# Building scratch sums in DRAM beside a projection: 1 MB accumulating DMAs with 8 KB rows, one in every second group, and copies seven to eight groups behind their sums

## The chip, the cores and the metric

One core of a Trainium2 chip. The time is the device time of one execution in microseconds (us); several executions are timed and the median is compared.

## The reference

One layer of a streaming encoder over 2048 prompt tokens and 64 sample tokens, float32, width 1024. Cut to what matters here:

```python
a = rmsnorm(h, norm1)
qa, ka, va, qr, kr, vr, gr = project(a, w_in)      # one projection, attention and retention columns
mixed = concat(window_attention(qa, ka, va), group_norm(retention(qr, kr, vr)) * silu(gr))
h = h + mixed @ w_out
u = relu(rmsnorm(h, norm2) @ w_up)                 # 1024 -> 4096
h = h + (u * u) @ w_down                           # 4096 -> 1024
y = rmsnorm(h, norm_f)
```

## The kernel before

The work has four stages, one after the other on TensorE.

1. **First projection with attention and retention.** Tokens are in tiles of 128 (17 tiles, the last of 64). The heads are done in two halves, `ph` 0 and 1, and for each half all tiles are gone through. A tile has three *groups* of matmuls (`ci` 0, 1, 2; lines 527, 528, 530), 102 groups in all; between the matmuls of a group stand the attention and retention steps of earlier tiles. The first and last tiles of each half are taken in pairs. The order on TensorE and on SyncE is written out by hand (`manual_schedule` for these two); that of the other engines is fixed when the program is built.
2. **Output projection** with residual and norm.
3. **Up projection** (`up_pair`, lines 856 to 858).
4. **Down projection** (lines 1025 to 1027) and last norm.

The two MLP products are done in the Strassen-Winograd way: weights and activations are cut into 2 x 2 blocks, and seven products of sums of blocks take the place of eight. For this, four sums of weight blocks are needed, with L11, L12, L21, L22 the blocks of a weight matrix: S1 = L21 + L22, S3 = L11 + L21, S2 = S1 + L11, S4 = S2 + L12. They do not depend on the tokens, and they are formed during stage 1 in DRAM scratch, `uscr` for w_up and `sscr` for w_down: a plain copy of one block into the scratch, issued from SyncE (line 585), and then an accumulating DMA that adds the other block to it, issued from GpSimd (POOL, line 588). Four copies and four sums make one unit; a unit is 512 KB of each sum, and there are 16.

`sum_step` has six steps for each unit, and the group loop calls them after the group with the number `first + 4 * u + 2 * k`:

- k = 0: copies S1 <- L21 and S3 <- L11; k = 1: sums S1 += L22, S3 += L21
- k = 2: copy S2 <- S1; k = 3: sum S2 += L11
- k = 4: copy S4 <- S2; k = 5: sum S4 += L12

So units overlap: away from the ends, every fourth group has four copies of 512 KB behind it, and two groups later there are four sums. On GpSimd a sum is placed behind the last rotation (`last_pool`, the addition of line 197). A copy that reads a sum (S2 <- S1, S4 <- S2) waits for it on SyncE, and a sum waits on GpSimd for the copy that it adds to.

On the same SyncE queue are, in program order, the loads of the next tiles: `load_x` (line 143, `xr`, one buffer), and `load_aux` (line 161, `rt`, the rotary table, two buffers; line 164, `xk`, the tokens for the norm, one buffer, in half 0 only). ScalarE squares `xk` (line 165) and splits `xr` into `xh` (line 154), GpSimd makes `xl` (line 155). GpSimd also forms `es` (line 291), the sink term of the softmax, which ScalarE then exponentiates (line 292).

In stages 3 and 4 `up_weights` (line 838) and `left` read single blocks from the weights and sums from the scratch. `wup` is laid out in 32 pieces of 128 rows of 1024 numbers, `uscr` in pieces of 128 rows of 512; `wdn` in 32 pieces `[128, 8, 128]`, by eights in one DMA; `sscr` in rows of 2048.

Of the kernel before, what the change touches and what calls it, by code (L numbers as in the profile page):

```python
# [11 lines left out]
F32 = mybir.dt.float32  # L12
F32R = mybir.dt.float32r
AF = mybir.ActivationFunctionType
ALU = mybir.AluOpType
# [24 lines left out]
def body(ctx, tc, xt, xtok, w1, wout, wup, wdn, gains, sinks, ck, cv, sret, rot, rdec, qdec, dmask,  # L40
         yT, nkp, nvp, nrp, nks, nvs, nrs):
    nc = tc.nc
# [3 lines left out]
    dp = ctx.enter_context(tc.tile_pool(name="scratch", bufs=1, space=DR))  # L46
# [3 lines left out]
    hscr = dp.tile([NK, 128, NTOK], F32, name="hscr")  # L50
    ascr = dp.tile([NP, 7, 128, 4, NB], F32, name="ascr")
    vscr = dp.tile([NP, 7, 128, 16, NB], F32, name="vscr")
    uscr = dp.tile([4, 16, 128, 512], F32, name="uscr")
    sscr = dp.tile([4, 4, 128, 2048], F32, name="sscr")

    idf = cp.tile([128, 128], F32, name="idf")
# [41 lines left out]
    last_pool = [None]  # L98
# [444 lines left out]
    S = NT - 1  # L543
# [8 lines left out]
    a, b = tiles[:2]  # L552
# [15 lines left out]
    def blocks(u):  # L568


        if u < 8:
            j = slice(2 * u, 2 * u + 2), slice(2 * u + 16, 2 * u + 18)
            return [uscr[k, j[0]].rearrange("j p c -> p j c") for k in range(4)], \
                [wup[e, :, c:c + 512].rearrange("j p c -> p j c") for e in j for c in (0, 512)]
        d, c = (u - 8) // 2, (u - 8) % 2 * 1024
        return [sscr[k, d, :, c:c + 1024] for k in range(4)], \
            [wdn[e].rearrange("p f n -> p (f n)")[:, a + c:a + c + 1024] for e in (d, d + 4) for a in (0, 2048)]

    def sum_step(u, k):

        (S1, S2, S3, S4), (L11, L12, L21, L22) = blocks(u)
        copies, sums = {0: ([(S1, L21), (S3, L11)], ()), 1: ((), [(S1, L22), (S3, L21)]), 2: ([(S2, S1)], ()),
                        3: ((), [(S2, L11)]), 4: ([(S4, S2)], ()), 5: ((), [(S4, L12)])}[k]
        for dst, src in copies:
            nc.sync.dma_start(dst, src)
        with tc.issue_after(last_pool[0].ins):
            for dst, src in sums:
                nc.gpsimd.dma_start(dst, src, accum_op=ALU.add, max_dma_last_dim=4096)

    first = groups.index((0, 2, 0))  # L590
    sums = {}
    for u in range(16):
        for k in range(6):
            sums.setdefault(first + 4 * u + 2 * k, []).append((u, k))
    aux = []

    for i, (ph, t, ci) in enumerate(groups):
# [13 lines left out]
        if aux and aux[0][0] <= i:  # L611
            u = aux.pop(0)[1]
# [32 lines left out]
    def rawslot(name):  # L645
        return wr.tile([128, 1024], F32, name=name, tag="wr")
# [7 lines left out]
    def split(h, l, x):  # L654
        nc.scalar.activation(h, x, AF.Copy)  # L655
        sub(l, x, h.bitcast(F32))  # L656
# [36 lines left out]
    RIGHT = {1: 0, 2: 1, 3: 2, 5: 3, 7: 4, 6: 5, 4: 6}  # L693

    LEFT = {5: 0, 6: 1, 7: 2, 3: 3}


    def load_mix(p, f):
# [46 lines left out]
    def norm_part(p, slot):  # L745

        n = Norm()

        def split():
            r, t = (slot(*x).rearrange("p (a n) t -> p a (n t)", a=2) for x in (("nr", F32R), ("nt", F32)))  # L750
            n.split(rs2[:, p * PN:p * PN + PN], accs[p], (r[:, 0], r[:, 1]), (t[:, 0], t[:, 1]))
        return split, n.sums, n.power
# [41 lines left out]
    with pool(name="op", bufs=1, side="right") as op:  # L794
# [7 lines left out]
        n = norm_part(0, opslot)  # L802
# [11 lines left out]
        n = norm_part(1, opslot)  # L814
# [17 lines left out]
    def up_weights(j):  # L832
        src = {}
        for n, i in enumerate(ORDER):
            if n % 2 == 0:
                r = rawslot("upr")
            x = r[:, n % 2 * 512:n % 2 * 512 + 512]
            nc.sync.dma_start(x, wup[j, :, :512] if i == 1 else wup[j, :, 512:] if i == 2 else
                              wup[j + 16, :, 512:] if i == 4 else uscr[LEFT[i], j])
            src[i] = x  # L840
        return src

    def up_pair(p, j, after):
        src = up_weights(j)
        a, b, c = psum("a"), psum("b"), zp.tile([128, 512], F32, name="c", tag="z")
        bank = {1: a, 2: a, 6: b, 7: b, 4: b, 5: c, 3: c}
# [65 lines left out]
    def left(i, d):  # L912

        out = []
        for g in range(2):
            r = rawslot("dr")
            if i in (1, 2, 4):
                e, a = d + 4 * (i == 4), 16 * (i != 1) + 8 * g
                nc.sync.dma_start(r.rearrange("p (f n) -> p f n", f=8), wdn[e, :, a:a + 8])
            else:  # L920
                nc.sync.dma_start(r, sscr[LEFT[i], d, :, g * 1024:g * 1024 + 1024])
            w = wd.tile([128, 2, 1024], F32R, name="wd", tag="wd")
            split(w[:, 0], w[:, 1], r)
            out.append(w)
        return out
# [78 lines left out]
    prods = [(p, i) for p in range(NP) for i in DOWN]  # L1004
    R = {prods[0]: [right(0, DOWN[0], c) for c in range(4)]}
    W = {steps[0]: left(*steps[0][1:])}
    pending = {}
    for n, (p, i, d) in enumerate(steps):
# [6 lines left out]
        if n + 1 < len(steps):  # L1015
            W[steps[n + 1]] = left(*steps[n + 1][1:])
# [36 lines left out]
        if last and i in (5, 3):  # L1053
            q = 22 if i == 5 else 12
            g = 4 * (q // 10 - 1) + d
# [29 lines left out]
def _rot_table():  # L1085
    pos = np.arange(NTOK).astype(np.float32)[:, None]
    out = []
    for f in (_FA, _FR):
        ang = (pos * f[None, :]).astype(np.float32).astype(np.float64)
        c, s = np.cos(ang), np.sin(ang)  # L1090
        out += [c, c, -s, s]
    return np.ascontiguousarray(np.concatenate(out, axis=1).astype(np.float32))


def _decay_tables():
    lg = _LOG_G.astype(np.float64)
    i = np.arange(128.0)
    rd = np.zeros((128, 2, 4))
    for a, C in enumerate((128, 64)):
        rd[:, a, :] = np.exp(lg[None, :] * (C - 1 - i)[:, None]) * 128.0 ** -0.5  # L1100
    qd = np.broadcast_to(np.exp(lg[:, None] * (i + 1)[None, :])[None], (128, 4, 128))
    causal = (i[None, :] >= i[:, None]).astype(np.float64)
    dm = np.concatenate([causal[:, None, :] * np.exp(-lg * C)[None, :, None] for C in (128, 64)], axis=1)
    return [np.ascontiguousarray(a.astype(np.float32)) for a in (rd, qd, dm)]
# [5 lines left out]
def _arrays(x_prompt, x_sample, cache_k, cache_v, state_ret, norm1, w_in, sinks, w_out, norm2, w_up, w_down, norm_f):  # L1110
    f = np.ascontiguousarray
    xa = np.concatenate([np.asarray(x_prompt)[0], np.asarray(x_sample)[0]], axis=0)
    xt = f(xa.T.reshape(8, 128, NTOK).transpose(1, 0, 2))
    w = np.asarray(w_in)[0]
    phs = []
    for ph in range(2):
        cols = [np.arange(640 + 64 * ph, 704 + 64 * ph),
                np.arange(256 * ph, 256 * ph + 256),
                np.arange(512 + 64 * ph, 576 + 64 * ph)]
        for b in (768, 1280, 1792, 2304):  # L1120
            cols.append(np.arange(b + 256 * ph, b + 256 * ph + 256))
        wp = w[:, np.concatenate(cols)]
        phs.append(wp.reshape(8, 128, WP).transpose(1, 0, 2))
    w1 = f(np.stack(phs, 0))
    wup = f(np.asarray(w_up)[0].reshape(8, 128, 32, 128).transpose(2, 1, 0, 3).reshape(32, 128, 1024))
    wout = f(np.asarray(w_out)[0].reshape(8, 128, 8, 128).transpose(2, 1, 0, 3).reshape(8, 128, 1024))
    wdn = f(np.asarray(w_down)[0].reshape(32, 128, 8, 128).transpose(2, 1, 0, 3))
    gains = f(np.stack([np.asarray(a).reshape(8, 128).T for a in (norm1, norm2, norm_f)], axis=1))
    sk = np.asarray(sinks)[0].reshape(2, 2, 2)
    sk = np.repeat(sk.transpose(2, 0, 1), 64, axis=0)  # L1130
    sk = f(np.concatenate([sk, sk], axis=2))
    rd, qd, dm = _decay_tables()
    return dict(xt=xt, xtok=f(xa), w1=w1, wout=wout, wup=wup, wdn=wdn,
                gains=gains, sinks=sk, ck=f(np.asarray(cache_k)[0, 0]), cv=f(np.asarray(cache_v)[0, 0]),
                sret=f(np.asarray(state_ret)[0, 0]), rot=_rot_table(), rdec=rd, qdec=qd, dmask=dm)
# [21 lines left out]
```

## Time and profile before

| | |
|---|---|
| median of 3 runs | 2346.11 us (2345.71 to 2350.67) |
| the profiled execution | 2352.45 us, its span 2350.7 us |
| busy share of the span | PE 95%, DVE 63%, ACT 47%, POOL 21% |
| DMA traffic | 515.91 MB, mean 219 GB/s |
| queue of SyncE (q1) | 470.21 MB, 59.5% of the DMA engines' time |
| queue of GpSimd (q0) | 43.43 MB, 10.0% |
| sums, `uscr` and `sscr` | 32 + 32 of 512 KB, median 10.8 and 10.9 us from issue to landing |
| granted TensorE clock | 0.973 of full speed |

Lines of the profile name the engine: PE is TensorE's matmul, PEld its weight load, ACT ScalarE, DVE VectorE, POOL GpSimd, SP SyncE; a q behind the name is that engine's instruction queue. `out<-in` are the program's names for tiles. In brackets stands how long the engine was idle before the instruction, and what ended that. "DMA to landing" is the time from the issue of a DMA to its completion. A busy engine costs time only where the chain of work passes through it, so the profile is read by stretches of time: the 40 slices of the page are 59 us each, and stage 1 fills the first 14.

### The profile page before, as it was taken

How to read it: one execution, taken by the hardware profiler on the slowest of the kernel's cores; microseconds unless marked ns; L12 is line 12 of the kernel's file. 1: busy time of each engine (PE TensorE's matmuls, PEld its weight loads, DVE VectorE, ACT ScalarE, POOL GpSimd, SP SyncE). 2: the span in 40 equal slices, each digit the busy share in tenths (PEclk: the TensorE clock that was granted, in tenths of full speed). 3: DMA queues.
4: the chain of work that ended last, by engine and by line, in shares of the span. 5: the costliest groups of instructions: out<-in, count | busy, mean ns of one | idle time of the engine just before them, and what ended most of it. 6: DMA issues, size and time to landing. Idle time of an engine off the chain costs nothing.

```text
span 2350.7 us, 35610 instructions
## 1 busy us (share of the span) xinstructions
PE 2241.2 (95%) x13256; PEld 2134.7 (91%) x13256; DVE 1469.8 (63%) x2460; ACT 1115.4 (47%) x1982; POOL 485.2 (21%) x582
## 2 busy tenths in 40 slices
PE   7978888898999989999999999999999999999998
PEld 5867777787888879999999999999999999999998
DVE  5544444554445565768768767766756776687665
ACT  5433333443334353345556556655644444444452
POOL 5544454443333322210000000000000110020012
PEclk9999898899999989999999999999999999999999
DMA  6557769885731277958979967876886677678762
GB/s 188 141 122 189 167 158 226 215 198 145 162 84 46 66 234 239 339 166 292 343 239 317 362 220 264 297 240 229 294 283 227 227 279 267 225 279 282 236 213 79
DMA packets 254766, 515.91 MB, mean 219 GB/s; under 512 B 22353, under 2 KB 128017, under 8 KB 254593
## 3 DMA queue, kind: packets, MB, share of 16 engines
q1 hardware_dynamic: 237312, 470.21, 59.5%
q0 software_dynamic: 17280, 43.43, 10.0%
q8 instruction: 104, 1.70, 0.3%
q14 instruction: 70, 0.57, 0.1%
HBM read 411.19 MB, written 169.54 MB: 247 GB/s over the span
## 4 chain that ended last, share of the span: by engine, by line
PE 83%; DMA 8%; ACT 2%; DVE 2%; POOL 2%; issue 1%; SPq 1%; DVEq 0%; POOLq 0%; ACTq 0%
PE y L1026 9%; PE y L1027 9%; PE y L1025 9%; PE z L527 5%; PE z L528 5%; PE z L530 4%; PE b L856 4%; PE b L857 4%; PE b L858 4%; DMA xk<-in_xtok 3%; PE y L731 3%; PE y L732 3%; PE c L856 3%; PE a L856 3%; PE a L857 3%; PE y L733 3%
## 5 line engine op out<-in xcount | busy, mean ns | idle before, releaser
L1026 PE MATMUL y<-vl,wd 128*128 128x352 f32 x1344 | 438.3, 326 | 0.0
L1027 PE MATMUL y<-vh,wd 128*128 128x352 f32 x1344 | 436.1, 324 | 1.3 <-DVE wd L656 1.3
L1025 PE MATMUL y<-vh,wd 128*128 128x352 f32 x1344 | 433.8, 323 | 2.7 <-ACT wd L655 2.7
L527 PE MATMUL z<-w,xh 128*128 128x512 f32 (+1 forms) x816 | 333.7, 409 | 12.3 <-ACT w L86 7.5
L976 POOL TENSOR_TENSOR acc<-acc,sq 128x352 f32<-128x352 f32 x41 | 73.0, 1780 | 1221.0 <-ACT sq L972 1221.0
L528 PE MATMUL z<-w,xh 128*128 128x512 f32 (+1 forms) x816 | 316.2, 387 | 1.3 <-DVE w L87 1.3
L655 ACT ACTIVATE wd<-dr 128x1024 fp32r<-128x1024 f32 x168 | 177.1, 1056 | 257.3 <-PE y L1027 187.7
L530 PE MATMUL z<-w,xl 128*128 128x512 f32 (+1 forms) x768 | 293.9, 383 | 1.6 <-POOL xl L155 1.6
L655 ACT ACTIVATE wu<-upr 128x512 fp32r<-128x512 f32 x336 | 209.4, 627 | 175.8 <-PE b L858 83.2
L656 DVE TENSOR_TENSOR wd<-dr,wd 128x1024 fp32r<-128x1024 f32 x168 | 209.3, 1247 | 110.8 <-ACT wd L655 103.0
L656 DVE TENSOR_TENSOR wu<-upr,wu 128x512 fp32r<-128x512 f32 x336 | 230.9, 693 | 69.4 <-ACT wu L655 54.3
L1025 PEld LDWEIGHTS y<-vh,wd 128*128 128x128 f32 x1344 | 254.5, 189 | 3.0 <-ACT wd L655 3.0
L1027 PEld LDWEIGHTS y<-vh,wd 128*128 128x128 f32 x1344 | 252.9, 188 | 1.6 <-DVE wd L656 1.6
L1026 PEld LDWEIGHTS y<-vl,wd 128*128 128x128 f32 x1344 | 252.8, 188 | 0.0
L527 PEld LDWEIGHTS z<-w,xh 128*128 128x128 f32 x816 | 161.0, 197 | 31.7 <-ACT w L86 7.9
L857 PE MATMUL b<-al,wu 128*128 128x352 f32 x576 | 185.9, 323 | 0.0
L856 PE MATMUL b<-ah,wu 128*128 128x352 f32 x576 | 185.8, 323 | 0.0
L858 PE MATMUL b<-ah,wu 128*128 128x352 f32 x576 | 185.5, 323 | 0.0
L528 PEld LDWEIGHTS z<-w,xh 128*128 128x128 f32 x816 | 160.5, 197 | 23.2 <-DVE w L87 4.9
L530 PEld LDWEIGHTS z<-w,xl 128*128 128x128 f32 x768 | 148.7, 194 | 25.9 <-POOL xl L155 2.1
L656 DVE TENSOR_TENSOR vl<-rv,vh 128x1408 fp32r<-128x1408 f32 x84 | 136.2, 1623 | 36.3 <-ACT vh L655 35.7
L655 ACT ACTIVATE vh<-rv 128x1408 fp32r<-128x1408 f32 x84 | 116.0, 1381 | 53.4 <-DMA rv<-vscr 33.2
(281 smaller groups left out, 4829.1 us busy)
## 6 DMA issues: line engine op xcount, KB each, us to landing
rv<-vscr SPq DMA_DIRECT2D x84, 704.0 KB, 5.4
vscr<-C SPq DMA_DIRECT2D x48, 1056.0 KB, 5.9
upr<-uscr SPq DMA_DIRECT2D x192, 256.0 KB, 4.8
dr<-sscr SPq DMA_DIRECT2D x96, 512.0 KB, 4.5
upr<-in_wup SPq DMA_DIRECT2D x144, 256.0 KB, 4.0
dr<-in_wdn SPq DMA_DIRECT2D x72, 512.0 KB, 4.8
uscr<-in_wup POOLq DMA_DIRECT2D x32, 512.0 KB, 10.8
sscr<-in_wdn POOLq DMA_DIRECT2D x32, 512.0 KB, 10.9
```

What stands on the lines that cost most here:

```text
L527: nc.tensor.matmul(z[:, :n], xh[:, k], wh, start=k == 0, stop=False)
L528: nc.tensor.matmul(z[:, :n], xh[:, k], wl, start=False, stop=k == NK - 1 and xl is None)
L530: nc.tensor.matmul(z[:, :n], xl[:, k], wh, start=False, stop=k == NK - 1)
L655: nc.scalar.activation(h, x, AF.Copy)
L656: sub(l, x, h.bitcast(F32))
L856: nc.tensor.matmul(o, wh, ah[:, k], start=k == 0 and i in (1, 6, 5), stop=False, skip_group_check=True)
L857: nc.tensor.matmul(o, wh, al[:, k], start=False, stop=False, skip_group_check=True)
L858: nc.tensor.matmul(o, wl, ah[:, k], start=False, stop=k == 3 and i in (2, 4, 3), skip_group_check=True)
L976: nc.gpsimd.tensor_add(self.acc, self.acc, sq)
L1025: nc.tensor.matmul(o, wh, vh, start=f == 0, stop=False)
L1026: nc.tensor.matmul(o, wh, vl, start=False, stop=False)
L1027: nc.tensor.matmul(o, wl, vh, start=False, stop=f == 15)
```

## The change

- The layouts of `wup`, `wdn` and both scratch tensors: each block becomes rows of 2048 numbers (8 KB), 128 rows for one unit. `wup` is `[4, 128, 16, 512]` and `wdn` `[4, 4, 128, 2048]`, with the first index the block (1, 2, 4 of the seven products are single blocks 0, 1, 3). The numbers in them are the same, put in order on the host.
- 8 units instead of 16. A sum is one accumulating DMA of 1 MB, with rows of up to 8 KB (`max_dma_last_dim`); a copy is two DMAs of 512 KB, half of each row.
- Units start every 8 groups, and each DMA has its own group: sums at +4, +6, +16, +26, which over all units is one in every second group; copies at +0, +2, +12, +23, their second halves one group later. S2 <- S1 comes 8 groups behind S1's sum, S4 <- S2 7 groups behind S2's.
- The later reads of single blocks and sums follow the new layouts: rows of 2 KB at a distance of 32 KB for the up projection, rows of 4 KB at 8 KB for the down projection.

```diff
-    uscr = dp.tile([4, 16, 128, 512], F32, name="uscr")
+    uscr = dp.tile([4, 128, 16, 512], F32, name="uscr")
...
     def blocks(u):
-        if u < 8:
-            j = slice(2 * u, 2 * u + 2), slice(2 * u + 16, 2 * u + 18)
-            return [uscr[k, j[0]].rearrange("j p c -> p j c") for k in range(4)], \
-                [wup[e, :, c:c + 512].rearrange("j p c -> p j c") for e in j for c in (0, 512)]
-        d, c = (u - 8) // 2, (u - 8) % 2 * 1024
-        return [sscr[k, d, :, c:c + 1024] for k in range(4)], \
-            [wdn[e].rearrange("p f n -> p (f n)")[:, a + c:a + c + 1024] for e in (d, d + 4) for a in (0, 2048)]
+        j = slice(4 * (u % 4), 4 * (u % 4) + 4)
+        return [[x[k, :, j].rearrange("p j c -> p (j c)") if u < 4 else x[k, u - 4] for k in range(4)]
+                for x in ((uscr, wup) if u < 4 else (sscr, wdn))]
...
+    COPIES = (("S1", "L21", 0), ("S3", "L11", 2), ("S2", "S1", 12), ("S4", "S2", 23))
+    SUMS = (("S1", "L22", 4), ("S3", "L21", 6), ("S2", "L11", 16), ("S4", "L12", 26))
+
+    def sum_step(u, dst, src, half):
+        S, L = blocks(u)
+        at = dict(zip(("S1", "S2", "S3", "S4", "L11", "L12", "L21", "L22"), S + L))
+        if half is None:
+            with tc.issue_after(last_pool[0].ins):
+                nc.gpsimd.dma_start(at[dst], at[src], accum_op=ALU.add, max_dma_last_dim=8192)
+        else:
+            c = slice(half * 1024, half * 1024 + 1024)
+            nc.sync.dma_start(at[dst][:, c], at[src][:, c])
...
-    for u in range(16):
-        for k in range(6):
-            sums.setdefault(first + 4 * u + 2 * k, []).append((u, k))
+    for u in range(8):
+        for dst, src, g in SUMS:
+            sums.setdefault(first + 8 * u + g, []).append((u, dst, src, None))
+        for dst, src, g in COPIES:
+            for half in range(2):
+                sums.setdefault(first + 8 * u + g + half, []).append((u, dst, src, half))
...
-            nc.sync.dma_start(x, wup[j, :, :512] if i == 1 else wup[j, :, 512:] if i == 2 else
-                              wup[j + 16, :, 512:] if i == 4 else uscr[LEFT[i], j])
+            nc.sync.dma_start(x, wup[PLAIN[i], :, j] if i in PLAIN else uscr[LEFT[i], :, j])
...
-            if i in (1, 2, 4):
-                e, a = d + 4 * (i == 4), 16 * (i != 1) + 8 * g
-                nc.sync.dma_start(r.rearrange("p (f n) -> p f n", f=8), wdn[e, :, a:a + 8])
-            else:
-                nc.sync.dma_start(r, sscr[LEFT[i], d, :, g * 1024:g * 1024 + 1024])
+            x = wdn[PLAIN[i], d] if i in PLAIN else sscr[LEFT[i], d]
+            nc.sync.dma_start(r, x[:, g * 1024:g * 1024 + 1024])
```

More of the change, by code (lines that the diff above doesn't have):

```diff
@@ L568, in blocks @@
     def blocks(u):
-        if u < 8:
-            j = slice(2 * u, 2 * u + 2), slice(2 * u + 16, 2 * u + 18)
-            return [uscr[k, j[0]].rearrange("j p c -> p j c") for k in range(4)], \
-                [wup[e, :, c:c + 512].rearrange("j p c -> p j c") for e in j for c in (0, 512)]
-        d, c = (u - 8) // 2, (u - 8) % 2 * 1024
-        return [sscr[k, d, :, c:c + 1024] for k in range(4)], \
-            [wdn[e].rearrange("p f n -> p (f n)")[:, a + c:a + c + 1024] for e in (d, d + 4) for a in (0, 2048)]
[L579 to L588, printed above, removed]
+        j = slice(4 * (u % 4), 4 * (u % 4) + 4)
[12 more added lines that the diff above has]
+            nc.sync.dma_start(at[dst][:, c], at[src][:, c])
     first = groups.index((0, 2, 0))
     sums = {}
-    for u in range(16):
-        for k in range(6):
-            sums.setdefault(first + 4 * u + 2 * k, []).append((u, k))
+    for u in range(8):
[4 more added lines that the diff above has]
+                sums.setdefault(first + 8 * u + g + half, []).append((u, dst, src, half))
     aux = []
@@ L695, in body @@
     LEFT = {5: 0, 6: 1, 7: 2, 3: 3}
+    PLAIN = {1: 0, 2: 1, 4: 3}
     def load_mix(p, f):
@@ L1124, in _arrays @@
     w1 = f(np.stack(phs, 0))
-    wup = f(np.asarray(w_up)[0].reshape(8, 128, 32, 128).transpose(2, 1, 0, 3).reshape(32, 128, 1024))
+    wup = f(np.asarray(w_up)[0].reshape(2, 4, 128, 2, 16, 128).transpose(3, 0, 2, 4, 1, 5).reshape(4, 128, 16, 512))
     wout = f(np.asarray(w_out)[0].reshape(8, 128, 8, 128).transpose(2, 1, 0, 3).reshape(8, 128, 1024))
-    wdn = f(np.asarray(w_down)[0].reshape(32, 128, 8, 128).transpose(2, 1, 0, 3))
+    wdn = f(np.asarray(w_down)[0].reshape(2, 16, 128, 2, 4, 128).transpose(3, 0, 4, 2, 1, 5).reshape(4, 4, 128, 2048))
     gains = f(np.stack([np.asarray(a).reshape(8, 128).T for a in (norm1, norm2, norm_f)], axis=1))
```

## The prediction

> **What bounds the kernel now.** I read the page first: busy shares over the span, and the chain that ended last.
>
> ```profile
> PE   7978888898999989999999999999999999999998
> ...
> PE 83%; DMA 8%; ACT 2%; DVE 2%; POOL 2%; issue 1%; SPq 1%; DVEq 0%; POOLq 0%; ACTq 0%
> ```
>
> TensorE (PE) bounds everything after slice 16. In slices 2 to 14 (59 us each), where the first projection runs and the scratch sums are built beside it, it is not full; the chain holds 8% DMA, although no transfer ought to end anything there. So the change is worth what this stretch loses, and I measure that by windows over line 527, which has 24 matmuls in each full token tile (8 for each of three groups):
>
> ```profile
> 72.70:138.20 65.50, 28.63 (x72) 13.60 (x72) 1.00 0.52 122
> 138.20:392.30 254.10, 89.59 (x216) 43.10 (x215) 0.89 0.73 174
> 392.30:491.80 99.50, 39.10 (x96) 19.11 (x97) 0.93 0.88 214
> 491.80:690.00 198.20, 78.39 (x192) 37.58 (x192) 0.94 0.63 147
> 690.00:795.00 105.00, 47.65 (x120) 22.66 (x120) 1.00 0.18 48
> ```
>
> The granted clock dips there too. Columns: stretch, its length, matmul and weight-load busy time of that line with their counts, clock, DMA share, GB/s. The last row is after the final sum: 120 matmuls, so 5 tiles, in 105.0 us: 21.0 us a tile, 7.0 a group, at full clock. Against this, 3 tiles in 65.5 lose 2.5 us, 9 in 254.1 lose 65.1, 4 in 99.5 (the change of head group, with new weights) lose 15.5, 8 in 198.2 lose 30.2. Together **113.3 us** are lost while sums run, idle time and lowered clock in one number. That is the most this change can give in this stage.
>
> Why it is lost, first from SyncE's own waits in 72 to 690 us, then from one case:
>
> ```profile
> SPq L585 <- DMA uscr<-in_wup: 172.4, 16, 25.4
> SPq L585 <- DMA sscr<-in_wdn: 118.3, 14, 25.0
> ```
>
> ```profile
> 88.88 0.42 SPq L164 DMA_DIRECT2D xk<-in_xtok  x1
> 97.61 0.55 SPq L585 DMA_DIRECT2D uscr<-uscr  x1
> ...
> 133.07 3.40 SPq L585 DMA_DIRECT2D uscr<-uscr  x2
> 140.37 2.08 SPq L164 DMA_DIRECT2D xk<-in_xtok  x1
> ```
>
> ```profile
> 89.80 2.45 POOL L588 DMA_DIRECT2D uscr<-in_wup  x2
> ```
>
> ```profile
> 149.47 1.06 ACT L154 ACTIVATE xh<-xr 128x1024 fp32r<-128x1024 f32 x1 [9.40 <-DMA xr<-in_xt]
> 157.33 0.45 PE L415 MATMUL prt<-idf,ro 128*128 128x128 f32 x1 [7.91 <-DVE ro L407]
> ```
>
> SyncE's queue stood 290.7 us at line 585, the copies that read a sum, 30 times. It runs ahead: it reaches the copy of 97.61 right behind the xk load of 88.88, while the sums this copy reads are only issued at 89.80 by GpSimd. Two groups of distance are eaten by its lead of about two groups, so it always waits until the sums land, with the next loads of xr, rt and xk behind it. At 133.07 it is let go, four copies (2 MB) go out first, xk only at 140.37; ScalarE stands 9.40 us for xr, and 7.91 us of PE are gone.
>
> There is a second way:
>
> ```profile
> 198.01 4.74 POOL L588 DMA_DIRECT2D uscr<-in_wup  x4
> 200.93 2.05 POOL L291 TENSOR_TENSOR es<-sk,ngm 128x4 f32<-128x4 f32 x1
> 205.99 0.21 ACT L292 ACTIVATE es<-es 128x4 f32<-128x4 f32 x1
> 208.40 0.47 PE L310 MATMUL pt<-idf,p 128*128 128x128 f32 x2 [2.55 <-DVE p L299]
> ```
>
> ```profile
> 707.35 0.20 POOL L291 TENSOR_TENSOR es<-sk,ngm 128x4 f32<-128x4 f32 x1 [0.17 <-DVE ngm L285]
> 708.89 0.21 ACT L292 ACTIVATE es<-es 128x4 f32<-128x4 f32 x1
> ```
>
> ```profile
> 204.60:214.10 9.50, 2.94 (x9) 1.64 (x9) 1.00 1.04 198
> 690.00:696.50 6.50, 2.96 (x9) 1.69 (x9) 1.00 0.53 121
> ```
>
> GpSimd issues four sums in 4.74 us, between its last rotation and es, the sink term of the softmax. Line 292 then comes 5 us behind line 291's start (1.5 us in the free tile, 707.35 to 708.89), PE waits 2.55 us, and that group takes 9.5 us where a free one takes 6.5: 3.0 us.
>
> **The change, part by part.**
>
> *Distance.* A copy comes 7 or 8 groups behind its sum, 49 to 56 us; less two groups of lead 35 to 42. The bursts of before:
>
> ```profile
> DMA to landing us min/median/max: 11.7/13.5/15.9
> DMA to landing us min/median/max: 3.9/7.9/11.7
> ```
>
> The first row is the burst's second to fourth sum, issued from 198.8 to 200.2; the second the copies of line 585. The second sum completes the first megabyte: it lands at 198.8 + 11.7 = 210.5, 12.5 us after the burst's first issue at 198.01, and I take that for one sum of 1 MB (bounds 11.7 and 15.9). The last lands at 200.2 + 15.9 = 216.1, so each further 512 KB takes (216.1 - 210.5)/2 = 2.8 us. All of it is far below 35, so the waits of 290.7 us go. Next in line at SyncE is the wait for a free rt buffer (line 161), which the free tiles have as well. In the other direction a sum comes 2 or 3 groups behind its copies (14 to 21 us, plus the lead) and these land within 11.7; GpSimd should not wait, and if it did, es, xl and the rotations would be behind it.
>
> *Whether neighbouring units wait for each other.* The new units interleave in memory (column blocks of one row). In before two units of sscr interleave in the same way, and the later one's copies were issued here:
>
> ```profile
> 400.38 1.99 SPq L585 DMA_DIRECT2D sscr<-in_wdn  x2
> DMA to landing us min/median/max: 11.0/12.3/15.9
> ```
>
> The second row is the sums issued from 386.8 to 388.1; the slowest of them, the last, landed near 404, after both copies had gone. So no wait over the whole block is seen; cost zero.
>
> *Size.* Bytes are the same, 64 copies of 512 KB stay 64, sums go from 64 to 32 of 1 MB.
>
> ```profile
> L588 POOL DMA_DIRECT2D uscr<-in_wup x32 | 38.1, 1787 | 0.0
> L588 POOL DMA_DIRECT2D sscr<-in_wdn x32 | 29.4, 1311 | 2.1 <-DMA sscr<-in_wdn 1.3 <-DMA sscr<-sscr 0.7
> ```
>
> sscr sums had 128 rows and 1.31 us, uscr sums 256 rows and 1.79; the new ones have 128 rows, so I take 1.31 (bounds 0 and 1.79): 42 us instead of 67.5, on an engine that is not the bound. What counts is one issue of 1.3 us ahead of es where 4.74 us stood: line 292 can follow its neighbours, and the 3.0 us go. ScalarE's order is fixed when the program is built, so this is my least certain step (rival 1).
>
> *Bursts.* Instead of 2 MB of copies and 2 MB of sums every four groups, one sum every second group and at most two copies in a group. The loads meet less:
>
> ```profile
> DMA to landing us min/median/max: 3.6/3.6/3.6
> 228.54 1.06 ACT L165 ACTIVATE xk<-xk 128x1024 f32<-128x1024 f32 x1 [1.33 <-DMA xk<-in_xtok]
> 228.60:249.60 21.00, 9.54 (x25) 4.54 (x25) 1.00 0.49 74
> 237.92 4.74 POOL L588 DMA_DIRECT2D uscr<-in_wup  x4
> 94.50:117.00 22.50, 9.45 (x24) 4.52 (x24) 1.00 0.68 179
> ```
>
> The first is the one xk load issued between 197 and 198 us, just ahead of the four sums of 198.01: 3.6 us, undisturbed. The second waits 1.33 us for xk, and yet its tile, the third row, takes 21.0 us (one matmul more lies on its edge), with the four sums of the fourth row issued inside. The fifth is the dearest tile without a long wait, 22.5. So what stays per tile lies between 0 and 1.5 us; I take 0.4, nearer the row that has a full burst in it, and for 27 tiles 11 us (bounds 0 and 40). The Trainium skill, DMA: Bandwidth & Descriptors, section Queues, rings and completion order, speaks against longer rows: each DMA engine serves its queues in turn and changes only when a packet is through. By that rule a load issued together with a sum would be late by all of the sum's time; the 3.6 us beside a burst do not agree.
>
> *Change of head group.* Its 15.5 us come partly from the same SyncE waits and partly from 6 MB of new weights. Bounds 0 and 15.5; with no row to split it I leave half, 8 us.
>
> *Reading the scratch later.* Rows of in_wup and uscr stay 2 KB, but 32 KB apart instead of 4 and 2; wdn rows go from 16 to 8 KB apart.
>
> ```profile
> upr<-uscr SPq DMA_DIRECT2D x192, 256.0 KB, 4.8
> upr<-in_wup SPq DMA_DIRECT2D x144, 256.0 KB, 4.0
> 1020.00:1670.00 650.00, 650.00 (x4063) 650.00 (x4063) 491.58 (x783) 383.42 (x543) 5.88 (x3) 1.00 0.79 271
> ```
>
> Rows 4 KB apart land no later than contiguous ones, and the up projection is full on PE with DMA at 0.79. Cost zero, covered by that fifth of DMA time (rival 3 if not).
>
> Sum: 113.3 - 11 - 8 = 94 us. The profiled execution took 2352.45 us (span 2350.7), 6.3 over the median; it would become 2258, and the median 2346.1 - 94 = **2252 us**. With everything gained it is 2233, with 40 and 15.5 left 2288: the forecast's own range.
>
> **The rivals.**
>
> 1. *The sink term stays late.* Every tile now has one sum right behind its second rotation. If the built order still puts line 292 behind the next xh, all 26 tiles pay 3.0 us: 78 instead of 11. Gain 27, time 2319. For it: that order is what cost the burst tiles; against it: 1.3 us ahead of es instead of 4.7.
> 2. *Loads caught in 8 KB rows.* xk is issued within 1 us of a sum. If its rows have to wait between the longer rows of the sum until that is through, it comes 2 x 2.8 = 5.6 us late; less the 1.3 us that cost nothing this is 4.3 in each of the 12 single tiles of the first head group, 52 us: 2304. Against it the 3.6 us beside four sums, though of shorter rows.
> 3. *Slower than before: the pitch of 32 KB.* In the up projection DMA works 0.79 x 650 = 513 us; its 336 weight loads are 88 of 176 MB, so some 257 us of that. If such rows took k times as long, DMA would pass 650 us at k = 1.53 and eat the whole gain at k = 1.9; at k = 2 it costs 120 us, 2372. Nothing in the rows points there. The Trainium skill, same page, section Latency and other measured facts, gives full rate at a pitch of 512 KiB and a loss from 2 MiB on, so it speaks against this rival; no trace here shows 32 KB.
> 4. *It does not do what it says:* the waits at line 585 stay, because of an order that I did not see (neighbour units). Then only the halved issue count is left: 2346, within 0.2%.
>
> **How the numbers follow.** Forecast (2233 to 2288) 0.68, rival 1 0.12, rival 2 0.09, rival 4 0.05, rival 3 0.06. A difference under 0.2% (5 us) is about what a measurement cannot tell from none. Forecast and rivals 1 and 2 are faster: 0.89; same 0.05; slower 0.06. The range goes from 2230 to 2315: forecast and rival 2, 0.77, with a part of rival 1.
>
> **What would show it.** SyncE's wait for sums at line 585 near zero; xk landing at 4 to 6 us in all tiles; 27 tiles at 21.0 to 21.5 us with granted clock 1.00; line 292 within 2 us of line 291; sums of 1 MB landing near 12.5 us with about 1.3 us of issue; up projection unchanged at 650 us. Wrong it becomes if GpSimd waits at line 588's successor, if xr or xk land late beside single sums, or if PE has gaps after 830 us that before does not have.

## The result and the profile after

The changed kernel takes **2261.9 us** (median of four runs, 2260.7 to 2264.4) against 2345.9 (2344.6 to 2350.7): a ratio of 0.964, 95% interval 0.9623 to 0.9656. The forecast was 2252 us, in a range of 2230 to 2315. The profiled execution took 2261.4 us, 91.1 less than that of before. Medians and ratios, here and below, leave out two executions with a lowered granted clock: one of e1 (2742.9 us at 0.747) and one of the kernel before that was run beside e5 to e8 (2495.2 us at 0.836).

The page of the changed kernel: busy tenths and granted clock in 40 slices, the chain that ended last, and the DMA issues (count, KB each, median us to landing).

```profile
PE   7999998999999999999999999999999999999998
PEclk9999998999999899999999999999999999999999
...
PE 93%; DMA 3%; DVE 1%; ACT 1%; POOL 1%; issue 1%; SPq 0%; DVEq 0%; ACTq 0%; POOLq 0%
...
uscr<-in_wup POOLq DMA_DIRECT2D x16, 1024.0 KB, 10.6
sscr<-in_wdn POOLq DMA_DIRECT2D x16, 1024.0 KB, 9.6
```

The thin slices of TensorE have gone but for the one of the turn (339 to 395 us, an 8), and the chain went from 83% PE and 8% DMA to 93% and 3%.

Where the time came from: line 527 again, the stage in which the scratch sums run, now cut at the starts of the same token groups in both kernels: twelve tiles of the first head group, four tiles around the change of head group (called the turn below), thirteen tiles of the second. Columns: stretch, its length, matmul and weight-load busy time of that line, clock, DMA share, GB/s. First before, then after:

```profile
72.73:392.34 319.61, 118.23 (x289) 56.73 (x288) 0.91 0.69 163
392.34:491.82 99.48, 39.09 (x96) 19.08 (x97) 0.93 0.88 215
491.82:795.06 303.24, 126.03 (x313) 60.27 (x312) 0.96 0.47 112
```

```profile
73.12:332.55 259.43, 114.24 (x288) 54.14 (x288) 1.00 0.68 186
332.55:429.99 97.44, 39.35 (x97) 19.29 (x97) 0.93 0.79 209
429.99:705.12 275.13, 123.77 (x312) 58.67 (x312) 1.00 0.56 143
```

The gain is 60.2 + 2.0 + 28.1 = 90.3 us, all but 0.8 of what the profiled executions differ by. The first and third stretch run at full clock; the turn gained next to nothing and keeps its clock of 0.93.

SyncE's own waits after, from 60 to 800 us, the first lines (us in total, times, longest):

```profile
SPq L161 <- DVE rot L196: 285.9, 27, 16.5
SPq L143 <- POOL p L263: 164.5, 20, 9.6
SPq L143 <- POOL xl L155: 52.6, 6, 13.5
```

The copies (now line 588) are not in the list at all, where before they stood in it with 290.7 us. SyncE now waits for free buffers of rt and xr, and that is harmless: it is ahead. The landing of xk in that stretch:

```profile
DMA to landing us min/median/max: 3.5/4.5/5.6
```

and a tile with copies (line 588) and a sum (line 585) inside, in order of time (start, duration, engine, line, tile; in brackets idle time before and its releaser):

```profile
198.32 0.50 SPq L588 DMA_DIRECT2D uscr<-in_wup  x1
198.78 0.94 POOL L585 DMA_DIRECT2D uscr<-in_wup  x1
199.43 0.51 POOL L291 TENSOR_TENSOR es<-sk,ngm 128x4 f32<-128x4 f32 x1
200.53 0.21 ACT L292 ACTIVATE es<-es 128x4 f32<-128x4 f32 x1
202.39 1.06 ACT L165 ACTIVATE xk<-xk 128x1024 f32<-128x1024 f32 x1 [1.15 <-DMA xk<-in_xtok]
```

Line 292 follows line 291 by 1.1 us (5 us before), right behind its own neighbours of line 288. What GpSimd pays for the sums (busy us, mean ns, idle before):

```profile
L585 POOL DMA_DIRECT2D uscr<-in_wup x16 | 14.8, 925 | 0.0
L585 POOL DMA_DIRECT2D sscr<-in_wdn x16 | 14.5, 904 | 0.0
```

No wait stands ahead of them, and 29.3 us of issue replace 67.5. The up projection, 650 us of it:

```profile
938.00:1588.00 650.00, 650.00 (x4063) 650.00 (x4063) 488.38 (x783) 386.58 (x544) 3.86 (x2) 1.00 0.80 273
```

The same 4063 matmuls as in the 650 us shown of before, at the same clock and a DMA share of 0.80 for 0.79.

### The profile page after: what moved, and what is told of

Same layout as the page of the kernel before. It is cut to its first block, busy times and chain, and to the rows that moved or that the text cites. A ratio compares the mean times of both kernels' runs of the same rounds, so it can differ in the third digit from the quotient of the medians.

```text
span 2259.6 us, 35535 instructions
## 1 busy us (share of the span) xinstructions
PE 2210.7 (98%) x13256; PEld 2110.8 (93%) x13256; DVE 1464.8 (65%) x2460; ACT 1113.7 (49%) x1982; POOL 447.1 (20%) x550
## 3 DMA queue, kind: packets, MB, share of 16 engines
q0 software_dynamic: 8576, 43.43, 9.1%
## 4 chain that ended last, share of the span: by engine, by line
PE 93%; DMA 3%; DVE 1%; ACT 1%; POOL 1%; issue 1%; SPq 0%; DVEq 0%; ACTq 0%; POOLq 0%
PE y L1026 10%; PE y L1027 10%; PE y L1025 10%; PE z L527 7%; PE z L528 7%; PE z L530 6%; PE b L860 4%; PE b L861 4%; PE b L859 4%; PE y L735 3%; PE y L736 3%; PE y L737 3%; PE a L860 3%; PE a L861 3%; PE a L859 3%; PE c L860 3%
## 5 line engine op out<-in xcount | busy, mean ns | idle before, releaser
L527 PE MATMUL z<-w,xh 128*128 128x512 f32 (+1 forms) x816 | 327.1, 401 | 12.9 <-ACT w L86 7.7
L528 PE MATMUL z<-w,xh 128*128 128x512 f32 (+1 forms) x816 | 311.1, 381 | 1.3 <-DVE w L87 1.3
L527 PEld LDWEIGHTS z<-w,xh 128*128 128x128 f32 x816 | 156.6, 192 | 32.3 <-ACT w L86 8.5
L528 PEld LDWEIGHTS z<-w,xh 128*128 128x128 f32 x816 | 156.5, 192 | 23.3 <-DVE w L87 5.4
## 6 DMA issues: line engine op xcount, KB each, us to landing
uscr<-in_wup POOLq DMA_DIRECT2D x16, 1024.0 KB, 10.6
```

The lines of the kernel that those rows point to most:

```text
L527: nc.tensor.matmul(z[:, :n], xh[:, k], wh, start=k == 0, stop=False)
L528: nc.tensor.matmul(z[:, :n], xh[:, k], wl, start=False, stop=k == NK - 1 and xl is None)
```

## The experiments

The total lay in the range; the question was which of the parts had earned it, since the prediction had priced the late sink term at 3.0 us a burst tile and left nearly all the rest to SyncE's waits. The theory at the start: distance is worth some 62 of the 84 us, spreading some 20. The rival: bursts cost more than es. In the table, the stretches are cut as above (us, from the profiled execution); the ratio is to the kernel before on the same chip.

| kernel | first half | turn | second half | sum | ratio, 95% interval |
|---|---|---|---|---|---|
| before | 319.6 | 99.5 | 303.2 | 722.3 | 1 |
| e1 far, bursts | 289.6 | 104.5 | 286.8 | 680.9 | 0.9836 (0.9815 to 0.9856) |
| e2 near, spread | 287.0 | 101.0 | 285.4 | 673.5 | 0.981 (0.9794 to 0.9827) |
| after: far, spread | 259.4 | 97.4 | 275.1 | 632.0 | 0.964 (0.9623 to 0.9656) |
| e3 rows of 4 KB | 260.0 | 95.2 | 275.1 | 630.4 | 0.9636 (0.962 to 0.9653) |
| e4 no scratch | 256.7 | 80.7 | 275.1 | 612.6 | 0.9543 (0.9529 to 0.9557) |
| e5 gap at the turn | 260.4 | 81.2 | 275.1 | 616.8 | 0.9555 (0.9539 to 0.9571) |
| e6 bursts at group 0 | 286.4 | 102.6 | 285.1 | 674.0 | 0.9826 (0.9806 to 0.9846) |
| e7 512 KB, spread | 262.6 | 101.6 | 280.7 | 644.9 | 0.9694 (0.9676 to 0.9711) |
| e8 1 MB, in pairs | 272.5 | 104.8 | 275.1 | 652.4 | 0.9692 (0.9674 to 0.971) |
| e9 bursts behind es | 275.2 | 101.7 | 300.9 | 677.8 | 0.9806 (0.9789 to 0.9822) |

**e1: distance alone.** The kernel before, its bursts and 512 KB units kept, with copies ten groups behind their sums.

```diff
-            sums.setdefault(first + 4 * u + 2 * k, []).append((u, k))
+            sums.setdefault(first + 4 * u + (0, 2, 12, 14, 24, 26)[k], []).append((u, k))
```

> The kernel before with one edit: copies that read a sum stand 10 groups behind it instead of 2, sums and copies still in bursts of four and units of 512 KB. My theory (two waits: SyncE at the copies, GpSimd's four issues ahead of es): the first goes, the second stays. Some 9 of 13 bursts of three or four sums stand right behind a tile's second rotation and cost 3.0 us each, 27 us; so about 2262 + 22 = 2284 us (2272 to 2298), PE waiting for p at line 310 for 20 us or more. Rival (size and row length make the gain): little is won, 2325 to 2346 us.

Measured: 2309.1 us (median of three, and the profiled execution), 25 over the forecast and outside its range. SyncE's waits at the copies went, as they were to, but the stage lost only 41.4 us. The chief waits of TensorE from 60 to 800 us:

```profile
PE pt L310 <- DVE p L299: 21.4, 7, 4.5
PE z L527 <- ACT xh L154: 14.1, 1, 14.1
PE pr L381 <- ACT vs L347: 9.0, 2, 6.0
```

The late sink term (line 310) is there as in before, 3.1 us for each of its 7 waits. The wait of 14.1 us, the longest, has another source. ScalarE stands ahead of it, in the second row here:

```profile
498.84 1.09 ACT L313 ACTIVATE ph<-pt 128x512 fp32r<-128x512 f32 x2 [1.70 <-PE pt L310]
509.69 0.38 ACT L417 ACTIVATE mr<-prt 128x256 f32<-128x256 f32 x1 [9.77 <-DMA mscr<-mr]
```

Line 417 writes mr, whose buffer comes free when line 418's store of it has landed; that small store goes through GpSimd's DMA queue, the one of the sums. It was issued behind four sums of 483.2 to 485.1 us, and in the chain of waits it is this step; the row below it is the landing time of these four sums (minimum, median, maximum):

```profile
490.78 18.83 DMA mscr<-mr
```

```profile
DMA to landing us min/median/max: 15.8/20.0/24.0
```

The last sum landed at 485.1 + 24.0 = 509.1, the store at 509.6. But the store was not alone. The load of xr that the same `xh` needs was issued on SyncE's queue at 490.67, 0.1 us before the store, and it is the slowest load of xr in e1 (minimum, median, maximum):

```profile
DMA to landing us min/median/max: 3.2/4.5/20.0
```

It landed at 510.67, and `xh` began at 511.48: without the late store at most 0.8 of the 14.1 us would have gone. So a burst does more than delay es: with four copies from SyncE beside it, a load and a small store that are issued after it land some 20 us late. Whether the store was held up by the sums ahead of it on its own queue, or like the load by the copies and sums in flight, this row does not tell; e6 has one that does.

**e2: spreading alone.** The changed kernel with its copies only two or three groups behind the sums they read.

```diff
-    COPIES = (("S1", "L21", 0), ("S3", "L11", 2), ("S2", "S1", 12), ("S4", "S2", 23))
-    SUMS = (("S1", "L22", 4), ("S3", "L21", 6), ("S2", "L11", 16), ("S4", "L12", 26))
+    COPIES = (("S1", "L21", 0), ("S3", "L11", 2), ("S2", "S1", 6), ("S4", "S2", 12))
+    SUMS = (("S1", "L22", 4), ("S3", "L21", 6), ("S2", "L11", 10), ("S4", "L12", 16))
```

> The changed kernel with one edit: copies that read a sum start 2 groups behind it (offsets +6 and +12; sums at +10 and +16), still 1 MB, 8 KB rows, one sum in every second group. My theory: SyncE waits again at 16 copies; 30 such waits cost some 92 us before, 3.1 each, so 50 us come back: about 2310 us (2290 to 2335). Rival (size and row length make the gain): it stays at 2262 us (2255 to 2270).

Measured: 2302.5 us, within the theory. SyncE's waits come back:

```profile
SPq L588 <- DMA uscr<-in_wup: 118.9, 8, 21.7
SPq L588 <- DMA sscr<-in_wdn: 96.8, 6, 22.1
```

With before and after this makes a square, in us of the stage: distance is worth 722.3 - 680.9 = 41.4 with bursts and 673.5 - 632.0 = 41.5 without; spreading in 1 MB units 48.8 at the near distance and 48.9 at the far. The two parts add up, and the second is far larger than the 20 us of the theory. It is more than spreading, though: between e1 and the changed kernel the size of the sums and the layout change too, and e7 splits them off.

**e3: row length.** The changed kernel with its sums cut into rows of 4 KB.

```diff
-                nc.gpsimd.dma_start(at[dst], at[src], accum_op=ALU.add, max_dma_last_dim=8192)
+                nc.gpsimd.dma_start(at[dst], at[src], accum_op=ALU.add, max_dma_last_dim=4096)
```

> The changed kernel with accumulating rows of 4 KB instead of 8 KB, nothing else. My theory: the row length does nothing, 2262 us (2256 to 2268). Rival A (long rows help): slower, 2275 us or more. Rival B (long rows hold up the loads between them): faster by 5 us or more.

Measured: 2264.0 us, no difference. GpSimd's queue on the two pages, after first, then e3 (packets, MB, share of 16 engines):

```profile
q0 software_dynamic: 8576, 43.43, 9.1%
```

```profile
q0 software_dynamic: 12672, 43.43, 9.5%
```

4096 packets more for the same bytes, hardly more engine time: the rows of 8 KB are worth nothing by themselves.

**e4: the floor.** The changed kernel without its scratch work: the sums are left out, and the later stages read plain blocks of the weights in their place, so its results are not the layer's.

```diff
-        for x in sums.pop(i, ()):
-            sum_step(*x)
+        sums.pop(i, ())
...
-            nc.sync.dma_start(x, wup[PLAIN[i], :, j] if i in PLAIN else uscr[LEFT[i], :, j])
+            nc.sync.dma_start(x, wup[PLAIN[i], :, j] if i in PLAIN else wup[LEFT[i], :, j])
...
-            x = wdn[PLAIN[i], d] if i in PLAIN else sscr[LEFT[i], d]
+            x = wdn[PLAIN[i], d] if i in PLAIN else wdn[LEFT[i], d]
```

> The changed kernel without any copy or sum in scratch; the later stages read plain weight blocks in place of the sums, so the MLP's numbers are not the reference's. It shows what the scratch traffic still costs. Of 22.7 us that the changed kernel's first stage loses against free tiles, 9.3 are in single tiles and 13.4 at the change of head group. If the latter comes from the scratch DMAs that meet the new weights (theory): 2242 to 2248 us. If it comes from the new weights alone (rival): 2251 to 2255 us.

Measured: 2240.9 us. Line 527 in the three stretches:

```profile
71.69:328.43 256.74, 114.24 (x288) 54.14 (x288) 1.00 0.27 79
328.43:409.13 80.70, 37.65 (x96) 18.23 (x97) 1.00 0.34 104
409.13:684.27 275.14, 123.78 (x313) 58.68 (x312) 1.00 0.17 47
```

So scratch work still costs the changed kernel 2.7 us in the first half, nothing in the second, and **16.7 us at the turn**. The new weights of the second head group, loaded here too, cost nothing when nothing else is in their way.

**e5: no scratch work at the turn.** The changed kernel with all copies and sums from token group 46 on moved nine groups later.

```diff
+    sums = {g + 9 * (g >= 46): x for g, x in sums.items()}
```

> The changed kernel; every copy and sum from group 46 on is placed 9 groups later, so that the change of head group (groups 46 to 54) has none; distances only grow. Without any scratch DMA the twelve groups 45 to 56 took 80.7 us, in the changed kernel 97.4. Theory (the new weights' loads share the DMA engines with scratch DMAs there): some 12 of these 16.7 us go, 2250 us (2244 to 2256). Rival (the cost moves with the DMAs to the groups behind): 2258 to 2265 us.

Measured: 2245.3 us (2243.0 to 2247.1), the fastest version that still does all the work. The turn's row:

```profile
335.15:416.39 81.24, 37.65 (x97) 18.23 (x97) 1.00 0.58 150
```

The turn takes 81.2 us, 0.5 over the floor, and the second half stays at 275.1, so the cost did not move with the transfers. From 345 to 396 us no copy or sum is issued; a sum at 344, one at 403 and a few copies from 396 on still lie inside the row. What was late there in the changed kernel is the first step of its chain from 355 to 405 us (start, us, what):

```profile
353.93 16.94 DMA w1raw<-in_w
```

A load of new weights that held the chain for 16.9 us beside copies and sums. The loads of new weights issued from 340 us on landed in 12.2 us at the median there, 18.6 at most; those of the turn in e5 in 4.9 and 7.5, in e4 in 5.3 and 7.6.

**e6: bursts kept, but away from es.** e1 with each burst of sums moved to the next token group with index 0 of its tile.

```diff
+            g = first + 4 * u + (0, 2, 12, 14, 24, 26)[k]
+            while k % 2 and groups[g][2]:
+                g += 1
+            sums.setdefault(g, []).append((u, k))
```

The edit does one thing more. The bursts of e1 stand four groups apart; moved to index 0 they stand three or six groups apart, and two of them meet in one group at the turn, eight sums in a row. The copies stay where they were, so that some come 6 groups behind their sums, not 10.

> The far-burst kernel (2312 us) with each burst of sums moved to the next group with ci = 0, behind the first rotation of a tile, where es does not follow. Theory (the burst's issues on GpSimd, ahead of es, hold up the softmax): the waits at line 310 for p (21.4 us, 7 times) go under 5 us and ph 1 is clean; but the sums are then in flight when xk is issued, so xk lands at 8 us instead of 4 in ph 0 and some of it comes back at line 381. About 2290 us (2275 to 2303). Rival (DMA traffic of a burst as such): unchanged at 2312 us (2305 to 2320), with the line 310 waits still there.

Measured: 2309.5 us, as slow as e1. Neither expectation fits as a whole: the time is the rival's, but the waits of line 310 are gone, as the theory had it. Others have their place, at line 381 above all; ScalarE's wait for the store of mr adds to them, twice:

```profile
PE pr L381 <- ACT vs L347: 27.3, 8, 6.9
PE pss L371 <- ACT rkT L365: 19.5, 4, 10.7
```

```profile
ACT mr L417 <- DMA mscr<-mr: 24.0, 2, 20.3
```

The longer of the two waits for a store is at the turn, behind the eight sums in a row, and TensorE's wait of 10.7 us follows from it. Its step in the chain of waits:

```profile
421.93 25.10 DMA mscr<-mr
```

The slowest of the four sums issued last, from 417.6 to 419.2 us, took 27.1 us and so landed by 446.3, and the store landed at 447.0, right behind it. A load of rt, 192 KB to the store's 128, was issued on SyncE's queue at 427.2, 5.3 us after the store, and landed at 436.8, 10 us before it. So here full DMA engines are not enough to explain the store's delay: it stood behind the sums on its own queue.

The other long stall comes from two bursts of sums, issued from 493.8 and from 512.8 us, three groups apart where e1 has four, with four copies between them. Stretches of 5 us (busy time of PE, weight loads, DVE, ACT and POOL with counts, then clock, DMA share, GB/s), and the step of the chain that came of it:

```profile
515.00:520.00 5.00, 5.00 (x37) 4.49 (x36) 2.99 (x9) 2.41 (x8) 4.18 (x7) 1.00 1.06 282
520.00:525.00 5.00, 5.00 (x31) 4.38 (x30) 2.98 (x8) 1.19 (x5) 0.20 (x1) 1.00 1.09 219
525.00:530.00 5.00, 5.00 (x29) 4.63 (x28) 1.35 (x6) 1.18 (x7) 0.00 (x0) 1.00 1.01 149
530.00:535.00 5.00, 0.24 (x2) 0.00 (x0) 0.00 (x0) 0.00 (x0) 0.00 (x0) 0.79 0.50 90
```

```profile
507.16 28.53 DMA xr<-in_xt
```

From 500 to 530 us the DMA engines are full; a load of xr issued among that lands after 28.5 us, and from 530 to 535 TensorE has two matmuls.

**e7: spread, but in 512 KB.** The layout and units of before, sums singly with at most one in a group, far behind.

```diff
-        copies, sums = {0: ([(S1, L21), (S3, L11)], ()), 1: ((), [(S1, L22), (S3, L21)]), 2: ([(S2, S1)], ()),
-                        3: ((), [(S2, L11)]), 4: ([(S4, S2)], ()), 5: ((), [(S4, L12)])}[k]
+        copies, sums = {0: ([(S1, L21), (S3, L11)], ()), 1: ((), [(S1, L22)]), 2: ((), [(S3, L21)]), 3: ([(S2, S1)], ()),
+                        4: ((), [(S2, L11)]), 5: ([(S4, S2)], ()), 6: ((), [(S4, L12)])}[k]
...
-            sums.setdefault(first + 4 * u + 2 * k, []).append((u, k))
+            sums.setdefault(first + 4 * u + (0, 2, 3, 11, 16, 25, 29)[k], []).append((u, k))
```

> The layout and the 512 KB units of before, but sums spread singly, one in every group, and copies that read a sum 9 groups behind it (S2) and 9 (S4). Theory (distance and spreading make the gain, size and row length none): 2262 us (2256 to 2272), although GpSimd has twice the issues. Rival (one sum of 1 MB is better than two of 512 KB at the same distance): 2275 us or more.

Measured: 2277.6 us, so the rival held. It splits the 48.9 us between e1 and the changed kernel: spreading alone, in units of 512 KB, gives 680.9 - 644.9 = 36.0, and the 1 MB units with their layout, half as many issues and one sum in every second group instead of every group give 644.9 - 632.0 = 12.9. By this, distance (41.4) and spreading (36.0) are near each other. What GpSimd pays in e7:

```profile
L588 POOL DMA_DIRECT2D uscr<-in_wup x32 | 39.5, 1329 | 0.4 <-issue 0.4
L588 POOL DMA_DIRECT2D sscr<-in_wdn x32 | 28.9, 958 | 0.9 <-DMA sscr<-in_wdn 0.8
```

**e8: 1 MB, but in pairs.** The changed kernel with two sums in one group, in every fourth group.

```diff
+    COPIES = (("S1", "L21", 0), ("S3", "L11", 2), ("S2", "S1", 14), ("S4", "S2", 25))
+    SUMS = (("S1", "L22", 6), ("S3", "L21", 6), ("S2", "L11", 18), ("S4", "L12", 34))
```

> The changed kernel with its 1 MB sums in pairs, two in every fourth group (offsets 6, 6, 18, 34; copies at 14 and 25, so 7 or 8 groups behind). Bytes, rows and distance as in the changed kernel, only the spreading is undone by half. Theory: 11 MB-long pairs keep the DMA engines busy for some 14 us after each pair, and GpSimd issues two (1.8 us) ahead of es instead of one (0.9): stalls come back in a part of the tiles, 2275 to 2290 us. Rival (spreading does not matter, distance and size do): 2262 us (2256 to 2268).

Measured: 2278.3 us, within the theory (a pair is two sums of 1 MB, 2 MB in all). Undoing half of the spreading gives back 16 us, with the layout, the size and the distance of the changed kernel: 13.1 in the first half, 7.3 at the turn in the profiled execution, none in the second half.

**e9: bursts behind es.** e1 with the bursts in the next group of index 2 and issued behind line 291 (here 292) instead of ahead of it. As in e6 this changes the spacing too: three to six groups between bursts, and eight sums in a row at the turn.

```diff
-        nc.gpsimd.tensor_add(es[:, :nu], sk[:, g, :nu], ngm[:, :nu])
+        last_es[0] = nc.gpsimd.tensor_add(es[:, :nu], sk[:, g, :nu], ngm[:, :nu])
...
-        with tc.issue_after(last_pool[0].ins):
+        with tc.issue_after(last_es[0].ins):
...
+            while k % 2 and groups[g][2] != 2:
+                g += 1
```

> The far-burst kernel (512 KB units, bursts of up to four sums, copies 10 groups behind; 2312 us) with each burst moved to the next group with ci = 2 and issued behind es instead of behind the last rotation: GpSimd is through with es, and xk was issued some us earlier. Theory (a burst costs by what it stands ahead of: es on GpSimd, and loads in flight): line 310 waits under 5 us, xk lands at 4 to 5 us, half 1 of the first stage (groups 57 to 96) falls from 286.8 to 275 to 278 us, half 0 (groups 9 to 45) from 289.6 to 260 to 272; the change of head group stays above 95. About 2282 us (2268 to 2292). Rival (a burst costs by its DMA work, wherever it stands: two bursts and their copies fill the DMA engines for 30 us, and a load issued in that time lands late): xr lands late, line 310 is clean, and the time stays at 2295 to 2312 us.

Measured: 2304.2 us, in the rival's range again. The sink term's wait (line 311 here) is not in TensorE's list; its longest waits are others. Lines are one higher here:

```profile
PE pss L372 <- ACT rkT L366: 14.5, 2, 10.7
PE pq L246 <- DVE hl L232: 12.4, 2, 7.2
PE pst L387 <- ACT p L289: 9.7, 1, 9.7
```

```profile
71.95:347.10 275.15, 115.19 (x288) 54.67 (x288) 0.98 0.67 168
...
448.83:749.76 300.93, 125.64 (x313) 59.83 (x312) 0.96 0.63 140
```

With es out of the way the first half gains 14.4 us over e1, and the second loses 14.1. The two placements that free the sink term (e6, e9) keep 42 and 46 us more in the stage than the changed kernel. Part of that may be the uneven spacing that both brought; bursts away from es at even distances were not run.

## Why the prediction was right, point by point

- **What the stage can give.** 113.3 us lost against tiles of 21.0 us. By the same measure the changed kernel still loses 632.0 - 29 x 21.0 = 23.0, so 90.3 were gained. The floor (e4) is 3.6 us above 29 such tiles: the measure was sound for the sum, though not stretch by stretch, since e4 lies 4.7 and 2.1 us above it in the halves and 3.3 below it at the turn.
- **Distance: no waits at the copies, SyncE next at line 161.** Right, by the waits shown, and by e2, where they return. Its size is 41 us.
- **The second way, 3.0 us in a burst tile by the late es.** This is the step that was mis-sized. The price itself held: 7 waits at line 310 in e1, 21.4 us, 3.1 each. But it is not all that a burst costs: spreading gives 36 us in units of 512 KB and 49 with the 1 MB units, and where the sink term was freed with the bursts kept, if unevenly spaced (e6, e9), the stage gained 7 and 3 us over e1. The prediction summed both ways in one number (113.3), so its total did not depend on the split, and came out although the split was wrong; the expectation of e1, which used it, missed by 25 us. What stands in its place: a burst fills the DMA engines and its own queue, so that loads of xr (20.0 us in e1, 28.5 in e6) and GpSimd's small stores of mr (18.8 us in e1, 25.1 in e6) are late, and with es out of the way the waits go to these. The prediction had looked at the loads beside a burst by the one xk of 3.6 us, which was issued ahead of its burst, and at the stores behind the sums not at all. How these us divide between es, loads and stores in the kernel before is open, since each placement of the bursts made waits of its own.
- **Line 292 close to line 291 (rival 1).** 1.1 us; rival 1 did not come.
- **Neighbouring units wait for each other: cost zero.** Right: 0.0 us of idle time at GpSimd's sums, no copies in SyncE's list. Rival 4 did not come.
- **Landing 12.5 us, issue 1.31 us for a sum of 1 MB.** Both too high: medians of 10.6 and 9.6 us, below the bound of 11.7, and 0.92 us. Neither decided anything.
- **Loads beside single sums (rival 2).** xk lands in 4.5 us at the median, 5.6 at most, where without scratch work (e4) it is 3.8 and 5.1: late by 0.7 at the median, not by the 5.6 of the rival. Rows of 4 KB (e3) make no difference to the time. The rule of the Trainium skill, DMA: Bandwidth & Descriptors, section Queues, rings and completion order, that a queue's turn lasts for a whole packet, had been weighed there: with rows half as long the time is 2264.0 for 2261.9, so the length of the rows made no time here; whether a turn lasts for a whole packet no run here shows.
- **What stays, 0.4 us in each of 27 tiles, 11 us.** 7.4 us in the first half and 2.1 in the second, 9.5 in all; but most of that is not scratch work: e4 keeps 4.7 and 2.1 of it. The tiles of the first half took 21.6 us on average, just over the 21.0 to 21.5 that were named, those of the second 21.2.
- **The turn: half of 15.5 us stays, for 6 MB of new weights.** 13.4 us stayed, and for another reason. Without scratch work the turn takes 80.7 us with the same weights; with scratch work kept out of most of it (e5) 81.2. So all of the 15.5 came with scratch work, and what the changed kernel keeps of it is scratch work meeting the loads of weights. This term, 5.4 us short, is most of the distance from a forecast gain of 94 to 90.3.
- **From the profiled execution to the median.** The forecast was 9.9 us too low, and the stage explains less than half of that. The 94 us were read from an execution 6.3 us longer than its median, but taken off the median. The profiled executions then differ by 91.1 us, the medians by 84.0: some 7 us of the gain are in the profiled executions alone.
- **Reading the scratch at a pitch of 32 KB (rival 3).** No cost: 650 us, DMA 0.80 against 0.79.

## What to carry to other kernels

Background transfers cost a busy stage in two ways that add up: a queue that runs ahead stands at the first transfer whose source isn't ready, with all later loads behind it, and a burst makes the loads beside it and the small stores behind it late, even where nothing waits for the burst itself. So put distance between dependent transfers by the queue's lead and not by the program's order, spread them evenly in few large pieces, and keep them out of the stretches where the kernel loads weights of its own; the last of these is worth 2261.9 - 2245.3 = 16.6 us here, in one line (e5). Moving a burst to a better place was no substitute here: in two attempts, both with the bursts set closer in places, the waits went elsewhere.

## What the runs showed of the hardware

- The packets of the accumulating DMAs cost mostly by their bytes here: 8576 and 12672 packets for the 43.43 MB of GpSimd's queue took 9.1% and 9.5% of the engines and the same device time.
- The issue of a sum on GpSimd took 0.92 us for 128 rows of 8 KB. Sums of sscr, 512 KB each, took 1.31 us in bursts (before) and 0.96 singly (e7): part of the price of before goes with issuing four in a row.
- A store of mr (128 KB) on GpSimd's queue took 25.1 us behind eight sums (e6), where 2.2 us is the least in that kernel, while a load of rt (192 KB) issued 5.3 us later on SyncE's queue took 9.6. The Trainium skill, DMA: Bandwidth & Descriptors, section Two DMAs through the same engine are not ordered, says that within one queue of one DMA engine descriptors start in order; these two times agree.
- A load could take 28.5 us (xr in e6) where the same load takes 4.4 at the median of that kernel, with the DMA engines full for 30 us; at the turn, new weights took 16.9 us beside scratch work.
- Line 293 on VectorE, an addition on 128x4 elements, took 1.20 us in a burst tile of before and 0.16 in a free one. Of its 31 instances in before from 60 to 800 us, eight took 0.28 to 2.04 us. Each of these met an operation of GpSimd on two tensors, seven times `xl` (line 155), and ended 0.01 to 0.03 us after it; here `xl` ran from 205.32 to 207.67. The other 23 met none and took 0.15 to 0.17 us. So a late es costs more by bringing line 293 beside `xl`, 1.0 us in the tile shown; in the changed kernel line 293 never met `xl`.

```profile
206.48 1.20 DVE L293 TENSOR_TENSOR sm<-sm,es 128x4 f32<-128x4 f32 x1
```
